# Preparation of out-projection weights tied behind TensorE's products; layer A's weight sums made in place and split a step later

## The chip, the cores and the metric

The kernel runs on one core of a Trainium2 chip. The metric is the device time of one execution in microseconds (us). The engines: PE (TensorE) multiplies, DVE (VectorE) and POOL (GpSimd) do elementwise work, ACT (ScalarE) evaluates functions and copies, SP issues transfers.

## The reference

```python
def recurrent_mixer(h, w_in, conv_w, conv_b, gate_w, gate_b, lam, w_out):   # layer A
    u = jnp.einsum('bsd,dc->bsc', h, w_in)                                  # in-projection
    gate, xb = u[..., :WIDTH], u[..., WIDTH:]
    xb = causal_depthwise_conv(xb, conv_w, conv_b)
    y = rg_lru(xb, gate_w, gate_b, lam)                                     # a scan over the sequence
    return jnp.einsum('bsc,cd->bsd', y * jax.nn.silu(gate), w_out)          # out-projection

def shortconv_mixer(h, w_in, conv_w, w_out):                                # layer B
    u = jnp.einsum('bsd,dc->bsc', h, w_in)                                  # four parts: bg, cg, xv, gate
    y = bg * causal_depthwise_conv(cg * xv, conv_w)
    return jnp.einsum('bsc,cd->bsd', y * jax.nn.silu(gate), w_out)

x = x + recurrent_mixer(rmsnorm(x, g0), ...)
x = x + shortconv_mixer(rmsnorm(x, g1), ...)
return rmsnorm(x, final_g)
```

The model width is 1024, the inner width 1536, the sequence 2048, all in float32.

## The kernel before, in words

**Stages.** Four projections follow one another on PE: A's in-projection (`in_A`), A's out-projection (`outA`), B's in-projection (`in_B`), B's out-projection (`outB`). Each float32 operand is split into two float16 tiles, a high part made by ACT and a remainder made by DVE, and each block product is three matmuls of 128x512 (`mm3`, L497, L500, L501). The sequence is cut into four chunks of 512 columns, called c = 0 to 3.

**Strassen's scheme.** The out-projections, and B's in-projection, use a seven-product scheme (`SEVEN`), which needs sums of weight blocks: S1 = A21 + A22, S2 = S1 - A11, S3 = A11 - A21, S4 = A12 - S2 (`combinations`, L473 and after; the sums themselves run on POOL at L481). The weights of an out-projection are therefore prepared during the in-projection before it and kept in DRAM: `OutSums.weights` loads four raw blocks for each of six k into tiles `wx` (four buffers, L1202), has POOL sum them into `ws` (two buffers, shared with junk of other squares), has `split_w` make the high part `wy` on ACT (L1189) and the remainder on DVE (L1190), and stores it (L1207). Before any of that it must know the scale of the weights: `out_scale` loads the 24 pieces of the whole matrix into `pre` and has ACT square and sum each (L816), then `scale_from` adds up (one small matmul `pt`, then L800 and other small DVE steps).

**How that work is spread.** These preparations are generators in the list `extra`. Each entry is [count, period, generator]; `advance`, called between pieces of the in-projection's products, adds one to the count and runs the generator a step whenever count % period is 0. For A the entry is [-60, 2, ...], for B [-24, 3, ...].

**What sets the order on an engine.** A scheduler orders the instructions of each engine by its own estimate of when each can run, and each engine then executes its list strictly in that order. `after(a, b)` only says that a stands behind b in the scheduler's time; it adds no wait. `pe_last` and `blocks_last` hold the newest product of PE. Many helpers tie their work behind it that way (`z_square`, `inv_between`), `out_scale`, `split_w` and the sums do not.

**in_A.** It goes pair by pair of heads (six pairs). A pair has two units: the first gives the convolution's input (evacuated by ACT L860 and DVE L862 to L871), the second the gate, evacuated by ACT L955 (Tanh) and DVE L956, which also frees the PSUM accumulators `acc` (six buffers, two for each run of 48 matmuls). The scan (`mixer`) runs ACT L908 to L926, POOL L929, DVE L930, and the products `z` go to DRAM through `z_done` (L761) with POOL's differences (L764) in the tiles `u` and `sg`.

**outA and the turn to in_B.** `emitA` takes each finished piece of x, squares it (ACT L226) and adds it to `sa` on POOL (L227). When a chunk c is complete, `endA` defers two steps by 2 and 4 products: the first puts the sum of squares through PE (`ss`, L233), the second broadcasts its inverse root through PE (`pn`, L259; copied to `inv` by ACT L262). `besideA` makes B's operands meanwhile: from product n = 52 it normalizes two of c = 2's eight blocks a step (L302). c = 3 is finished in `second_half`, at the start of in_B: its `ss` and `pn`, then eight L302, then differences and splits by L348, L354, L364, L368 and L310. `unit_scale` for the next unit's weights ends with DVE L394, and the splits L417 (ACT) and L418 (DVE) wait for it.

Of the kernel before, what the change touches and what calls it, by code (L numbers as in the profile page):

```python
# [10 lines left out]
AF = mybir.ActivationFunctionType  # L11
ALU = mybir.AluOpType
# [6 lines left out]
NH = 12  # L19
CH = 512  # L20
HALF = 1024
KB = D // P
# [24 lines left out]
def trunk(ctx, tc, xT, xn, prm, wa, ga, oa, wb, ob, out):  # L47
    nc = tc.nc
    v, s, g, sp = nc.vector, nc.scalar, nc.gpsimd, nc.sync
# [17 lines left out]
    wt = {  # L67
        (l, n, k): dr.tile([P, 2, CH], F16, name=f"w{l}{n}_{k}", tag=f"w{l}{n}_{k}")
        for l, names in (("A", ("S1", "S2", "S3", "S4")), ("B", ("A11", "A12", "A22", "S1", "S2", "S3", "S4")))
        for n in names  # L70
        for k in range(NH // 2)
    }
# [19 lines left out]
    def buf(pool, tag, name, bufs, dt=F32):  # L92
        return pool.tile([P, ROW], dt, tag=tag, name=name, bufs=bufs)[:, 0:CH]

    def pair16(pool, tag, name, bufs):
        t = pool.tile([P, 2, ROW], F16, tag=tag, name=name, bufs=bufs)
        return t[:, :, 0:CH]
# [4 lines left out]
    def two_over(dst, src):  # L102

        v.tensor_scalar(
            out=dst.bitcast(I32), in0=src.bitcast(I32), scalar1=EXP_MASK, scalar2=None,
            op0=ALU.bitwise_xor,
        )
# [4 lines left out]
    def root(dst, src):  # L112

        v.tensor_scalar(out=dst, in0=src, scalar1=TINY, scalar2=None, op0=ALU.max)
        v.tensor_scalar(
            out=dst.bitcast(I32), in0=dst.bitcast(I32), scalar1=1, scalar2=EXP_MASK,
            op0=ALU.logical_shift_right, op1=ALU.bitwise_and,
        )
# [170 lines left out]
    def inv_between(acc, inv, queue=None):  # L289

        ss = ps.tile([P, 4], F32, tag="g", name="ss", bufs=2)[:, 0 : acc.shape[1] // P]
        with tc.high_priority(PR):
            sums_of(acc, ss, pe_last[0])
        if not queue:
            yield
        with tc.high_priority(PR):
            inv_from(ss, inv, queue, s.copy, pe_last[0])
        yield


    def normed(l, x, kk, inv):
        return v.scalar_tensor_tensor(  # L302
            out=x, in0=x, scalar=gs[l][:, kk : kk + 1], in1=inv, op0=ALU.mult, op1=ALU.mult
        )
# [79 lines left out]
    def unit_scale(l, sq, sw, behind=None):  # L384


        pt = ps.tile([P, 4], F32, tag="g", name="pt", bufs=2)
        ins = nc.tensor.matmul(pt, ones, sq, start=True, stop=True)
        if behind is not None:
            after(ins, behind)  # L390
        v.tensor_reduce(out=sw[:, 0:1], in_=pt, axis=AX.X, op=ALU.add)  # L391
        root(sw[:, 1:2], sw[:, 0:1])
        two_over(sw[:, 2:3], sw[:, 1:2])
        v.tensor_scalar(  # L394
            out=sw[:, 2:3], in0=sw[:, 2:3], scalar1=0.5 * W_TOP / ROOT, scalar2=None, op0=ALU.mult
        )
        v.tensor_scalar(
            out=sw[:, 3:4], in0=sw[:, 1:2], scalar1=hs[l], scalar2=ROOT,
            op0=ALU.mult, op1=ALU.mult,
        )  # L400
        return sw
# [74 lines left out]
    def combinations(raw):  # L476


        def wsum(x, y, op):
            t = buf(wp, "ws", "ws", 2)  # L480
            g.tensor_tensor(out=t, in0=x, in1=y, op=op)  # L481
            return t

        a11, a12, a21, a22 = raw
        yield "A11", a11
        s1 = wsum(a21, a22, ALU.add)
        yield "S1", s1
        s2 = wsum(s1, a11, ALU.subtract)
        yield "S2", s2
        yield "A12", a12  # L490
        yield "S4", wsum(a12, s2, ALU.subtract)
        yield "S3", wsum(a11, a21, ALU.subtract)
        yield "A22", a22
# [9 lines left out]
    throttle, pe_last, blocks_last, evac_last = [None, None], [None], [None], [None]  # L503
# [136 lines left out]
    def defer(fn, steps):  # L640
        deferred.append([steps, fn])
# [9 lines left out]
    extra = []  # L651
# [141 lines left out]
    def scale_from(sq, t, behind=None):  # L793


        pt = ps.tile([P, 2 * NH], F32, tag="g", name="pt", bufs=2)[:, 0 : sq.shape[1]]
        ins = nc.tensor.matmul(pt, ones, sq, start=True, stop=True)
        if behind is not None:
            after(ins, behind)
        v.tensor_reduce(out=t[:, 1:2], in_=pt, axis=AX.X, op=ALU.add)  # L800
        root(t[:, 1:2], t[:, 1:2])
        two_over(t[:, 0:1], t[:, 1:2])
        v.tensor_scalar(
            out=t[:, 0:1], in0=t[:, 0:1], scalar1=0.5 * W_TOP / ROOT, scalar2=None, op0=ALU.mult
        )
        v.tensor_scalar(
            out=t[:, 1:2], in0=t[:, 1:2], scalar1=ROOT / W_TOP, scalar2=None, op0=ALU.mult
        )

    def out_scale(wdram, t):  # L810

        sq = wsq
        for i in range(2 * NH):
            b = buf(wp, "ws", "pre", 2)
            sp.dma_start(b, wdram[:, i * CH : (i + 1) * CH])
            s.activation(b, b, AF.Square, accum_out=sq[:, i : i + 1])  # L816
            if i < 2 * NH - 1:
                yield
        scale_from(sq, t)
        yield  # L820

    marks = []
# [256 lines left out]
    def in_order(ins):  # L1079

        if loads:
            after(ins, loads[-1])
        loads.append(ins)

    def after(ins, first):
        tc.add_manual_dep(
            ins.ins, first.ins.name,
            mybir.DependencyInfo(mybir.DependencyClass.NoSync, mybir.DependencyReason.SCHED_ONLY),
            reason="order",
        )  # L1090
# [45 lines left out]
    class OutSums:  # L1136
# [49 lines left out]

        def split_w(self, pool, tag, bufs, a):
            t = pair16(pool, tag, tag, bufs)
            s.activation(t[:, 0, :], a, AF.Copy, scale=self.wsc[:, 0:1])  # L1189
            v.scalar_tensor_tensor(  # L1190
                out=t[:, 1, :], in0=a, scalar=self.wsc[:, 0:1], in1=t[:, 0, :],
                op0=ALU.mult, op1=ALU.subtract,
            )
            return t

        def weights(self, pre):

            yield from pre
            for k in range(KH):
                raw = []  # L1200
                for n in range(4):
                    raw.append(buf(wk, "wx", "wx", 4))  # L1202
                    sp.dma_start(raw[n], self.raw_w(k, n))
                yield
                for name, a in combinations(raw):
                    if (self.l, name, k) in wt:
                        sp.dma_start(wt[self.l, name, k], self.split_w(wk, "wy", 2, a))  # L1207
                        yield
                    if self.l == "A" and name == "S3":
                        break  # L1210

        def load_z(self, half, name, k):
            t = self.raw[half, name, k] = buf(wp, "zr", "zr", 10)
# [166 lines left out]
    for c in range(2):  # L1380
        for i in range(4):
            t = wk.tile([P, D], F32, tag="xn", name="xn", bufs=4)
# [31 lines left out]
    sideA = [second()]  # L1414

    preA, preB = out_scale(oa, wsc[0]), out_scale(ob, wsc[1])

    def follows(l, wdram, t):

        o = OutSums(l, wdram, t)  # L1420

        def start(anchor):
            o.start(anchor)
            extra.append([0, 1, o.ahead()])
        return o, start
# [3 lines left out]
            run(extra.pop(0)[2])  # L1429

    outA, startA = follows("A", oa, wsc[0])
    extra.append([-60, 2, outA.weights(preA)])
    in_A(hA, w0, head, sideA, startA, nothing)
    while sideA:
        advance(sideA)
# [18 lines left out]
    def endA(c, ts):  # L1454
        if c == 3:
            return
        steps = inv_between(sums[c], inv[c // 2][c % 2])
        for n in (2, 4):
            defer(lambda: next(steps, None), n)

    def besideA(n):


        if n in (1, 5):
            raw = []
            u = n // 4
            for q in range(4):
                raw.append(buf(wk, "wx", "wx", 4))
                in_order(sp.dma_start(raw[q], wb[u][:, q * CH : (q + 1) * CH]))
            sws.append(unit_scale(1, *unit_squares(raw), pe_last[0]))  # L1470
        if n >= 32 and n < 36:
            k = n - 32
            for kk, name in ((k, "B11"), (k + 4, "B21")):
                normed(1, xh[0][kk, 0], kk, inv[0][0])
                add(hB[0], name, k, xh[0][kk, 0])
        if n == 35:
            for ks in ((0, 1), (2, 3)):
                early.append(build_h(1, xh[0], inv[0], ks, hB[0], (0,)))
            early.append(unit_weights(1, wb[0], w0, sws[0]))
        if n >= 52:  # L1480
            for kk in range(2 * n - 104, 2 * n - 102):
                normed(1, xh[1][kk, 0], kk, inv[1][0])
        while early and next(early[0], "end") == "end":
            early.pop(0)

    outA.run(emitA, endA, besideA)
    x = xh[1]
    while early:
# [214 lines left out]
```

## Time and profile before

| | |
|---|---|
| median of 3 runs | 1977.35 us (1976.88 to 1980.92) |
| the profiled execution | 1978.52 us, of which span 1976.7 us |
| busy in the span | PE 98%, DVE 65%, ACT 56%, POOL 36% |
| mean granted clock of PE | 0.992 of full speed |
| PE's longest waits | 6.5 us (DVE L956), 5.3 us (at the start), 3.6 us (DVE L871), 3.0 us (POOL L227) |

The table is read from the last row up: PE is busy for nearly the whole span, so what another engine does matters only where PE stands still for it, or runs at a lower clock. The profile has a list of such waits, and a column PEclk in its table by stretches: 1.00 there is 2.4 GHz, 0.50 is 1.2 GHz.

### The profile page before, as it was taken

The numbers are of one execution on the slowest core, as the hardware profiler recorded it, in microseconds if no ns is written. First come the engines' busy times: TensorE is split into PE (matmuls) and PEld (weight loads), VectorE is DVE, ScalarE is ACT, GpSimd is POOL, SyncE is SP. The second block draws the span as 40 slices with busy tenths as digits, with TensorE's granted clock in tenths as the row PEclk, the third lists the DMA queues.
The fourth block names the chain that finished last, engine by engine and source line by source line (L and its number), as shares of the span: only waits on it lengthen the run. The fifth ranks groups of instructions, "written<-read, shape, count | busy, mean of one in ns | idle before, by whom it ended". The sixth has DMA issues, their size and how long they took to land.

```text
span 1976.7 us, 25501 instructions
## 1 busy us (share of the span) xinstructions
PE 1936.4 (98%) x8930; PEld 904.1 (46%) x8930; DVE 1278.6 (65%) x2098; ACT 1099.9 (56%) x1968; POOL 707.6 (36%) x554
## 2 busy tenths in 40 slices
PE   8999989999999999999999999999999999999998
PEld 4444434444444444444444444444444444444446
DVE  7978877866667787979536656647636336544565
ACT  6888768676757563555644454454452443544432
POOL 0023533221212130344553583664553443522221
PEclk9999999999999999999999999999999999999999
DMA  8432442221104985421241241342130030397472
GB/s 300 140 101 86 152 142 88 84 75 48 70 22 175 386 328 181 149 96 59 70 150 37 81 165 43 97 144 72 62 117 28 27 112 27 122 371 247 109 227 86
DMA packets 157713, 250.88 MB, mean 127 GB/s; under 512 B 15248, under 2 KB 58896, under 8 KB 157584
## 3 DMA queue, kind: packets, MB, share of 16 engines
q1 hardware_dynamic: 157360, 248.72, 37.5%
q8 instruction: 70, 1.15, 0.2%
q0 software_dynamic: 224, 0.53, 0.1%
q14 instruction: 59, 0.48, 0.1%
HBM read 171.06 MB, written 78.12 MB: 126 GB/s over the span
## 4 chain that ended last, share of the span: by engine, by line
PE 79%; DVE 3%; DMA 0%; ACT 0%; issue 0%; POOL 0%; SPq 0%; DVEq 0%; ACTq 0%; POOLq 0%
PE acc L497 11%; PE acc L500 11%; PE acc L501 11%; PE p L501 8%; PE p L497 8%; PE p L500 8%; PE r L497 4%; PE r L500 4%; PE r L501 4%; PE pg L904 2%; PE q L500 2%; PE q L501 2%; PE q L497 2%; DVE op L310 1%; PE ss L233 0%; DMA wr<-in_wb 0%
## 5 line engine op out<-in xcount | busy, mean ns | idle before, releaser
L497 PEld LDWEIGHTS <-wc 128*128 128x128 f16 x2096 | 207.8, 99 | 261.4 <-issue 18.3
L500 PEld LDWEIGHTS <-wc 128*128 128x128 f16 x2096 | 205.3, 98 | 265.8 <-issue 32.8
L501 PEld LDWEIGHTS <-wc 128*128 128x128 f16 x2096 | 205.3, 98 | 257.8 <-issue 15.1
L497 PE MATMUL acc<-op,wc 128*128 128x512 f16 x752 | 284.2, 381 | 14.8 <-DVE sg L956 8.7
L497 PE MATMUL p<-op,wc 128*128 128x512 f16 x768 | 290.8, 379 | 1.4 <-ACT wc L417 1.2
L500 PE MATMUL p<-op,wc 128*128 128x512 f16 x768 | 291.1, 379 | 0.0
L501 PE MATMUL p<-op,wc 128*128 128x512 f16 x768 | 290.6, 379 | 0.4 <-DVE wc L418 0.4
L500 PE MATMUL acc<-op,wc 128*128 128x512 f16 x752 | 286.2, 381 | 2.2 <-DVE op L310 2.2
L501 PE MATMUL acc<-op,wc 128*128 128x512 f16 x752 | 286.2, 381 | 0.0
L929 POOL TENSOR_TENSOR u<-fixed,u 128x512 f32<-128x512 f32 x48 | 54.0, 1147 | 347.4 <-ACT fixed L926 347.4
L227 POOL TENSOR_TENSOR sa<-sa,sq 128x512 f32<-128x512 f32 x48 | 71.0, 1480 | 273.1 <-ACT sq L226 225.9
L1294 DVE SCALAR_TENSOR_TENSOR xo<-acc,fixed,xo 128x512 f32<-128x512 f32 (+1 forms) x120 | 85.0, 710 | 113.2 <-PE acc L501 112.3
L418 DVE SCALAR_TENSOR_TENSOR wc<-wr,fixed,wc 128x512 f16<-128x512 f32 x122 | 105.3, 881 | 78.8 <-ACT wc L417 73.5
L418 DVE SCALAR_TENSOR_TENSOR wc<-ws,fixed,wc 128x512 f16<-128x512 f32 x104 | 104.0, 1005 | 80.4 <-ACT wc L417 72.4
L501 PE MATMUL r<-op,wc 128*128 128x512 f16 x384 | 145.5, 379 | 0.0
L500 PE MATMUL r<-op,wc 128*128 128x512 f16 x384 | 145.5, 379 | 0.0
L497 PE MATMUL r<-op,wc 128*128 128x512 f16 x384 | 145.5, 379 | 0.0
L993 POOL TENSOR_TENSOR pb<-pb,cg 128x512 f32<-128x512 f32 x48 | 69.0, 1437 | 188.6 <-DVE fixed L391 101.9
L417 ACT ACTIVATE wc<-wr,fixed 128x512 f16<-128x512 f32 x122 | 83.6, 712 | 82.1 <-DVE fixed L394 79.5
L862 DVE SCALAR_TENSOR_TENSOR u<-acc,fixed,u 128x511 f32<-128x511 f32 (+2 forms) x138 | 100.8, 741 | 43.5 <-ACT u L860 43.5
L379 ACT ACTIVATE junk<-wr 128x512 f32<-128x512 f32 x136 | 84.3, 621 | 31.8 <-DMA wr<-in_wa 16.1
L930 DVE TENSOR_TENSOR_SCAN u<-a,fixed,u 128x512 f32<-128x512 f32 x48 | 78.5, 1638 | 35.4 <-POOL u L929 35.4
(209 smaller groups left out, 3926.9 us busy)
## 6 DMA issues: line engine op xcount, KB each, us to landing
wr<-in_wb SPq DMA_DIRECT2D x104, 256.0 KB, 3.6
zAT<-u SPq DMA_DIRECT2D x48, 256.0 KB, 2.0
zr<-zAT SPq DMA_DIRECT2D x48, 256.0 KB, 5.1
zr<-zBT SPq DMA_DIRECT2D x48, 256.0 KB, 5.1
wr<-in_wa SPq DMA_DIRECT2D x44, 256.0 KB, 4.2
zAB<-sg SPq DMA_DIRECT2D x36, 256.0 KB, 2.0
zr<-zAB SPq DMA_DIRECT2D x36, 256.0 KB, 5.4
zBB<-ed SPq DMA_DIRECT2D x36, 256.0 KB, 2.0
```

The costliest lines, as they stand in the source:

```text
L227: squared[0] = eng.tensor_tensor(out=acc, in0=acc, in1=sq, op=ALU.add)
L379: ins = s.activation(junk, t, AF.Square, accum_out=sq[:, m : m + 1])
L417: last_hi[0] = s.activation(t[:, 0, :], src, AF.Copy, scale=sw[:, 2:3])
L418: v.scalar_tensor_tensor(out=t[:, 1, :], in0=src, scalar=sw[:, 2:3], in1=t[:, 0, :], op0=ALU.mult, op1=ALU.subtract,)
L497: ins = nc.tensor.matmul(acc, wh, xh, start=start, stop=False, **kw)
L500: nc.tensor.matmul(acc, wh, xl, start=False, stop=False, **kw)
L501: return nc.tensor.matmul(acc, wl, xh, start=False, stop=stop, **kw)
L862: v.scalar_tensor_tensor(out=u[:, n:], in0=a[:, 0 : CH - n], scalar=ac(3 - n), in1=u[:, n:], op0=ALU.mult, op1=ALU.add,)
L929: g.tensor_tensor(out=u, in0=w, in1=u, op=ALU.mult)
L930: v.tensor_tensor_scan(out=u, data0=a, data1=u, initial=stA[:, h : h + 1], op0=ALU.mult, op1=ALU.add,)
L993: g.tensor_tensor(out=t, in0=t, in1=cg[m, half, c], op=ALU.mult)
L1294: ins = v.scalar_tensor_tensor(out=x[:, ts], in0=acc[:, ts], scalar=zsc[half][:, 2:3], in1=x[:, ts], op0=ALU.mult, op1=ALU.add,)
```

## The change

Four edits. `now` puts an instruction behind the newest product of PE in the scheduler's time: `out_scale`'s squares, `split_w`'s ACT copy, and A's sums get it, and `scale_from` is given the same and a step of its own. For layer A `sums_only` makes the four sums in place, on POOL, in the tiles of the raw weights (S1 in a22, S3 in a21, S2 in a11, S4 in a12), in two steps of two, and the four splits follow in the next four steps; a k takes seven steps in place of five. `endA` defers 3 and 5 products in place of 2 and 4 for c = 1 and 2. c = 2's blocks are normalized from n = 53, three a step.

```diff
+    def now(ins):
+        last = pe_last[0] or blocks_last[0]
+        if last is not None:
+            after(ins, last)
 ...
-            s.activation(b, b, AF.Square, accum_out=sq[:, i : i + 1])
-            if i < 2 * NH - 1:
-                yield
-        scale_from(sq, t)
+            now(s.activation(b, b, AF.Square, accum_out=sq[:, i : i + 1]))
+            yield
+        scale_from(sq, t, pe_last[0] or blocks_last[0])
         yield
 ...
         def split_w(self, pool, tag, bufs, a):
             t = pair16(pool, tag, tag, bufs)
-            s.activation(t[:, 0, :], a, AF.Copy, scale=self.wsc[:, 0:1])
+            now(s.activation(t[:, 0, :], a, AF.Copy, scale=self.wsc[:, 0:1]))
 ...
                 yield
-                for name, a in combinations(raw):
-                    if (self.l, name, k) in wt:
+                for name, a in self.sums_only(raw) if self.l == "A" else combinations(raw):
+                    if name:
                         sp.dma_start(wt[self.l, name, k], self.split_w(wk, "wy", 2, a))
-                        yield
-                    if self.l == "A" and name == "S3":
-                        break
+                    yield
+
+        def sums_only(self, raw):
+            a11, a12, a21, a22 = raw
+            def to(x, a, b, op):
+                now(g.tensor_tensor(out=x, in0=a, in1=b, op=op))
+            to(a22, a21, a22, ALU.add)
+            to(a21, a11, a21, ALU.subtract)
+            yield None, None
+            to(a11, a22, a11, ALU.subtract)
+            to(a12, a12, a11, ALU.subtract)
+            yield None, None
+            yield from (("S1", a22), ("S3", a21), ("S2", a11), ("S4", a12))
 ...
-    extra.append([-60, 2, outA.weights(preA)])
+    extra.append([-30, 2, outA.weights(preA)])
 ...
-        for n in (2, 4):
+        for n in (3, 5) if c else (2, 4):
 ...
-        if n >= 52:
-            for kk in range(2 * n - 104, 2 * n - 102):
+        if n >= 53:
+            for kk in range(3 * n - 159, min(KB, 3 * n - 156)):
```

Every engine has as many instructions of each kind as before; only their order differs. The start count -30 in place of -60 moves nothing: the period is 2, and count % 2 is 0 for every second step of a negative count too, so in both kernels the generator starts at once.

**ACT, pair hp = 1 of in_A.** Here stand the evacuations L955 of the pair's gate unit, the mixer's L926, and the splits `wy` of the out-projection's weights. Before (L1189 is `split_w`):

```order
L955 ACTIVATE sg<-acc,fixed 128x512
L1189 ACTIVATE wy<-ws,fixed 128x512
L955 ACTIVATE sg<-acc,fixed 128x512
L926 ACT_TABLE_LOAD
L926 ACTIVATE fixed<-fixed 128x1024
L1189 ACTIVATE wy<-ws,fixed 128x512
L786 ACTIVATE fixed<-sg 128x512 x2
L1189 ACTIVATE wy<-ws,fixed 128x512 x2
L379 ACTIVATE junk,fixed<-wr 128x512
L1189 ACTIVATE wy<-ws,fixed 128x512
L955 ACT_TABLE_LOAD
L955 ACTIVATE sg<-acc,fixed 128x512 x2
```

Changed (the changed file has other line numbers: L960 is L955 of before, L931 is L926, L1194 is L1189, L865 is L860):

```order
L931 ACT_TABLE_LOAD
L931 ACTIVATE fixed<-fixed 128x1024
L960 ACT_TABLE_LOAD
L960 ACTIVATE sg<-acc,fixed 128x512 x2
L1194 ACTIVATE wy<-wx,fixed 128x512
L786 ACTIVATE fixed<-sg 128x512 x2
L1194 ACTIVATE wy<-wx,fixed 128x512
L960 ACTIVATE sg<-acc,fixed 128x512 x2
L1194 ACTIVATE wy<-wx,fixed 128x512
L786 ACTIVATE fixed<-sg 128x512 x2
L1194 ACTIVATE wy<-wx,fixed 128x512
L865 ACTIVATE u<-acc,fixed 128x512 x2
```

Of the five splits shown between the first L955 and the last two, two stay ahead of the last two. From the first split of the kernel to that place there were eleven, now there are two; the others come later in in_A, the last in the fifth pair, where before it stood in the fourth.

**POOL, the same place.** L764 are the differences of z, L929 the mixer's products, L481 the sums. Before:

```order
L929 TENSOR_TENSOR u<-fixed,u 128x512 x6
L481 TENSOR_TENSOR ws<-wx 128x512
L764 TENSOR_TENSOR u<-sg 128x512
L481 TENSOR_TENSOR ws<-wx 128x512
L764 TENSOR_TENSOR u<-sg,u 128x512
L764 TENSOR_TENSOR u<-sg 128x512
L481 TENSOR_TENSOR ws<-ws,wx 128x512
L764 TENSOR_TENSOR u<-sg,u 128x512
L481 TENSOR_TENSOR ws<-wx,ws 128x512
L481 TENSOR_TENSOR ws<-wx 128x512
L929 TENSOR_TENSOR u<-fixed,u 128x512 x2
L481 TENSOR_TENSOR ws<-wx 128x512
```

Changed (L934 is L929 of before, L1220 the sums in place):

```order
L934 TENSOR_TENSOR u<-fixed,u 128x512 x6
L1220 TENSOR_TENSOR wx<-wx 128x512 x2
L764 TENSOR_TENSOR u<-sg 128x512 x2
L764 TENSOR_TENSOR u<-sg,u 128x512
L1220 TENSOR_TENSOR wx<-wx 128x512
L764 TENSOR_TENSOR u<-sg,u 128x512
L1220 TENSOR_TENSOR wx<-wx 128x512
L934 TENSOR_TENSOR u<-fixed,u 128x512 x2
L764 TENSOR_TENSOR u<-sg 128x512 x2
L764 TENSOR_TENSOR u<-sg,u 128x512 x2
L1220 TENSOR_TENSOR wx<-wx 128x512 x4
L934 TENSOR_TENSOR u<-fixed,u 128x512 x4
```

In both, the sums share POOL's list with the mixer and the differences. Between the two groups of mixer's products the changed list has four sums, the old one five; the old one has three more at once after the second group, the changed one four, but only behind the four differences.

**PE, the end of outA.** `ss` of c = 2, among the products of S1 (`wv` are its weights; each `acc` takes 18 matmuls). Before:

```order
L497 LDWEIGHTS wv_7112
L497 MATMUL acc_7367<-zs_6872,wv_7112 128x512
L500 LDWEIGHTS wv_7112
L500 MATMUL acc_7367<-zs_6872,wv_7112 128x512
L501 LDWEIGHTS wv_7112
L501 MATMUL acc_7367<-zs_6872,wv_7112 128x512
L233 MATMUL ss_7362<-fixed_310,sa_7071 128x1 x4
```

Changed:

```order
L497 LDWEIGHTS wv_7136
L497 MATMUL acc_7338<-zs_6989,wv_7136 128x512
L500 LDWEIGHTS wv_7136
L500 MATMUL acc_7338<-zs_6989,wv_7136 128x512
L501 LDWEIGHTS wv_7136
L501 MATMUL acc_7338<-zs_6989,wv_7136 128x512
L233 MATMUL ss_7365<-fixed_310,sa_7047 128x1 x4
```

Both pieces stand in the third accumulator of S1: before, `ss` follows its first three matmuls, the 39th of the run; now it follows all 18, the 54th.

## Rows read from the trace of the kernel before

**Rows 1.** The page: busy time, share of the span, instructions.
```profile
PE 1936.4 (98%) x8930; PEld 904.1 (46%) x8930; DVE 1278.6 (65%) x2098; ACT 1099.9 (56%) x1968; POOL 707.6 (36%) x554
```
**Rows 2.** Whom PE waited for: us in total, times, longest us.
```profile
PE acc L497 <- DVE sg L956: 8.7, 2, 6.5
...
PE acc L497 <- DVE u L871: 3.6, 1, 3.6
PE ss L233 <- POOL sa L227: 3.0, 1, 3.0
...
PE pt L388 <- DVE sg L956: 0.9, 1, 0.9
```
**Rows 3.** Stretches: length, busy us (instructions) of PE, PEld, DVE, ACT, POOL; PEclk, DMA, GB/s.
```profile
127.00:129.00 2.00, 0.00 (x0) 0.00 (x0) 2.00 (x5) 0.72 (x2) 1.34 (x2) 1.00 1.04 400
225.00:250.00 25.00, 21.28 (x99) 9.53 (x98) 20.48 (x20) 17.78 (x35) 21.45 (x13) 1.00 0.61 201
250.00:275.00 25.00, 21.87 (x87) 9.29 (x87) 14.98 (x34) 11.96 (x22) 6.70 (x5) 0.86 0.39 131
825.00:850.00 25.00, 22.01 (x95) 10.84 (x94) 20.60 (x25) 12.20 (x22) 15.83 (x11) 0.86 0.34 116
850.00:875.00 25.00, 25.00 (x122) 11.87 (x120) 18.37 (x28) 12.11 (x21) 10.38 (x7) 1.00 0.38 126
875.00:925.00 50.00, 48.34 (x229) 22.15 (x227) 48.95 (x77) 31.00 (x63) 18.71 (x14) 1.00 0.12 37
...
1000.00:1430.00 430.00, 429.81 (x2010) 196.81 (x2009) 251.06 (x346) 204.33 (x396) 235.66 (x187) 1.00 0.29 95
```
**Rows 4.** Timeline of PE after 252: start, us, instruction, [idle before <-releaser].
```profile
252.77 0.59 PE L497 MATMUL acc<-op,wc 128*128 128x512 f16 x1 [6.49 <-DVE sg L956]
...
257.37 0.38 PE L501 MATMUL acc<-op,wc 128*128 128x512 f16 x1
```
**Rows 5.** Timeline of ACT, 245 to 252.
```profile
245.46 0.72 ACT L1189 ACTIVATE wy<-ws,fixed 128x512 f16<-128x512 f32 x1 [3.25 <-POOL ws L481]
247.59 0.72 ACT L1189 ACTIVATE wy<-ws,fixed 128x512 f16<-128x512 f32 x1 [1.41 <-POOL ws L481]
...
251.31 1.27 ACT L955 ACTIVATE sg<-acc,fixed 128x512 f32<-128x512 f32 x2
```
**Rows 6.** Timeline of DVE, 242 to 253.
```profile
242.25 4.25 DVE L930 TENSOR_TENSOR_SCAN u<-a,fixed,u 128x512 f32<-128x512 f32 x2
...
252.03 1.28 DVE L956 SCALAR_TENSOR_TENSOR sg<-sg,acc 128x512 f32<-128x512 f32 x2 [1.25 <-ACT sg L955]
```
**Rows 7.** POOL's instructions by line: names, shapes, count, busy us, mean ns, idle before.
```profile
L227 POOL TENSOR_TENSOR sa<-sa,sq 128x512 f32<-128x512 f32 x48 | 71.0, 1480 | 273.1 <-ACT sq L226 225.9 <-DMA zr<-zAB 44.3 <-DMA xo<-x 2.6
...
L481 POOL TENSOR_TENSOR ws<-wx 128x512 f32<-128x512 f32 x24 | 36.3, 1511 | 36.2 <-ACT junk L379 24.7 <-DMA wx<-in_oa 6.9 <-PE p L501 3.8
```
**Rows 8.** Timeline of PE, 826 to 845, outA's last products.
```profile
826.12 0.38 PE L497 MATMUL acc<-zs,wv 128*128 128x512 f16 x1
...
834.32 0.38 PE L501 MATMUL acc<-zs,wv 128*128 128x512 f16 x1
837.69 1.87 PE L233 MATMUL ss<-fixed,sa 128*128 128x1 f32 x8 [2.99 <-POOL sa L227]
839.42 0.59 PE L497 MATMUL acc<-zs,wv 128*128 128x512 f16 x1
...
844.45 0.38 PE L497 MATMUL acc<-zs,wv 128*128 128x512 f16 x1
```
**Rows 9.** Timeline of POOL, the last addition to c = 2's squares.
```profile
836.00 1.64 POOL L227 TENSOR_TENSOR sa<-sa,sq 128x512 f32<-128x512 f32 x1 [2.02 <-ACT sq L226]
```
**Rows 10.** Timeline of DVE, 879 to 917, start of in_B.
```profile
879.37 5.83 DVE L302 SCALAR_TENSOR_TENSOR xo<-xo,fixed,inv 128x512 f32<-128x512 f32 x8 [0.52 <-ACT inv L262]
...
916.91 0.13 DVE L394 TENSOR_SCALAR fixed<-fixed 128x1 f32<-128x1 f32 x1
```
**Rows 11.** Timeline of PE, 917 to 918.
```profile
917.85 0.39 PE L497 MATMUL p<-op,wc 128*128 128x512 f16 x1 [1.23 <-ACT wc L417]
```

## The prediction

> **What bounds the kernel now.** I read the page's busy times first: PE works for 98% of the span [rows 1], so the change can only win where PE stands still or runs at its lower clock. The list of PE's waits comes next [rows 2]. The reader is to see four of its lines: 8.7 us in two waits for DVE's L956, 3.6 us in one for L871, 3.0 us in one for POOL's L227, and 0.9 us more for L956. Then the table by stretches, for PEclk [rows 3]: 1.00 but for 0.86 in 250 to 275 and in 825 to 850, the stretches behind two of those waits; a stretch at 1.2 GHz follows them. Last come the timelines of the engines named there. Three places matter.
>
> *246 us.* PE stands still for 6.49 us until DVE's L956 frees an accumulator, and then issues 11 matmuls from 252.77 to 257.37, 0.42 us apart [rows 4]. At the full clock 39 matmuls start between 826.12 and 834.32, so one takes 8.20 / 38 = 0.216 us [rows 8]; the 11 lost 4.60 - 11 x 0.216 = 2.2 us. L956 at 252.03 waited for ACT's L955 at 251.31 [rows 5, 6], and L955 stood in ACT's list behind splits L1189, which waited for sums of POOL: 3.25 and 1.41 us at the last of them [rows 5]. So the place costs 6.5 + 2.2 = 8.7 us.
>
> *332 us.* The other wait for L956: 8.7 - 6.5 = 2.2 us [rows 2].
>
> *834 us.* PE reaches c = 2's `ss` after 39 of the S1 products and waits 2.99 us for the last addition to its squares [rows 8, 9]. Afterwards the clock is at the lower level: 12 matmuls from 839.42 to 844.45 cost 5.03 - 12 x 0.216 = 2.4 us too much, and the eight small passes of `ss`, 837.69 to 839.42, half of their 1.73 us, 0.9 [rows 8]. That place costs 3.0 + 3.3 = 6.3 us.
>
> **The change part by part.**
>
> *Layer A's splits and sums.* Nothing is added or removed: 24 sums on POOL, 24 splits on ACT and DVE. The trace has no sum of `wx` in place, but L227 writes over one of its inputs and takes 1480 ns against 1511 for the sums [rows 7], so I take the same duration. What moves is the order. Nine of the eleven splits ahead of the last pair of L955 go: 9 x 0.72 = 6.5 us, and with them the waits of 4.7 us [rows 5]. By that alone L955 would run at 251.3 - 11.2 = 240.1. Two things keep it later: two splits remain ahead of it, and the evacuations before it stand behind the mixer's L926, which has its own chain. I estimate 241 to 243.5. On DVE, L956 follows the two scans (4.25 us together [rows 6]) and two L1190, so it ends at 243 to 246. PE needs the accumulator 6.49 us before 252.77, at 246.28. So the wait goes, and the slow stretch with it; I leave 0.7 us for a remainder: +8.0 us. The ends are +8.7 and, if L956 comes 3 us later than I think and the clock falls again, +3.
>
> *What is late next in A.* The removed splits come back in the third to fifth pair. At 332 us ACT's order up to the awaited L955 is the same as before, its splits ahead are two fewer, and it starts from an earlier end of the second pair: +1.5 of 2.2 us, with ends 2.2 and -2. In the first pair the squares of the raw weights move ahead of an evacuation L860, and both L882 of the pair ahead of an L862, on the chain that ends in the 3.6 us of L871 [rows 2]; each of these costs DVE or ACT 0.6 to 0.7 us. I take -0.8 us, ends +0.5 and -1.7. The splits in the fourth and fifth pair, 13 of them, fall where PE did not wait at all: -0.8 us, ends 0 and -2. Of the 0.9 us that PE waited for L956 at a `pt` [rows 2], in the second pair too, I count +0.6. Layer A together: 8.0 + 1.5 - 0.8 - 0.8 + 0.6 = +8.5 us.
>
> *outA's end.* `ss` of c = 2 now stands after 54 of the S1 products instead of 39. The 15 more take 15 x 0.216 = 3.2 us, from 834.70 (where PE stopped, 837.69 - 2.99) to 837.94; POOL's addition ends at 836.00 + 1.64 = 837.64 [rows 9]. So the wait is covered by 0.3 us, the products themselves being the cover, and in_B would start 6.3 us earlier. If POOL is later by up to 1 us, that much comes back, but a pause so short leaves the clock up, as 2.2 us at 332 did.
>
> *But this gain meets a full DVE.* From 875 to 925 DVE is busy 48.95 of 50 us, against 18.37 of 25 us before it [rows 3]. The stretch runs from the first L302 at 879.37 to L394 at 916.91, 37.5 us [rows 10]; PE stands still for 1.23 us and starts at 917.85, 0.94 us after L394 [rows 11]. L302 waits for `pn` of c = 3. Its place in PE's order is seven matmuls later than before (1.5 us), and PE is 6.3 us earlier, so L302 starts at 879.4 - 6.3 + 1.5 = 874.6. Between L302 and L394 the order has one L540 and one L418 fewer and two L1029 more: as many instructions, 0 to 1.7 us longer, I take 1.0. L394 then comes at 874.6 + 37.5 + 1.0 = 913.1, PE starts at 914.0 and not at 917.85: of 6.3 us 3.8 remain, and PE's wait there grows from 1.2 to about 3.7 us. The ends: 4.8 us if DVE's extra is nothing, and 0 if DVE can't start L302 before 879 because its list before it is as full.
>
> *Does the clock fall after a wait of 3.7 us?* The rows disagree: it fell after 6.49 and after 2.99 us, and stayed at 1.00 in and after the 3.6 us for L871 [rows 2, 3]. I take that it stays, and keep -2.5 us as an end. The Trainium skill (TensorE: Matmul & The Clock Gate, "Why this matters for your kernels") warns against pauses between bursts of matmuls, since TensorE then starts again at the lower clock. By that rule the new wait pays the same price as the old one at 834 us, and the gain at this place shrinks to some 1 us; this case's rows follow the rule at 246 and 834 us and not at the wait for L871.
>
> *The normalizing of c = 2 in threes from n = 53, `ss` of c = 1 18 matmuls later.* PE waited at neither; eight L302 in three steps instead of four are the same work on a DVE that has 6.6 us of idle time in 850 to 875 [rows 3]. I take 0, ends +0.3 and -1.
>
> *B's ties.* The combinations of layer B stay as they are; ACT's squares and splits are ordered a little differently throughout in_B. There PE is busy for 429.81 of 430 us [rows 3], so nothing can be won. I take -0.7 us, ends 0 and -3.
>
> Sum: 8.5 + 3.8 - 0.7 = 11.6 us less than the profiled execution's own 1978.52, 1966.9. That execution was 1.2 us above the median of 1977.35, which gives 1965.7; I forecast 1966.3, between.
>
> **The rivals.**
>
> *The second gain is spent.* DVE can't start L302 earlier, or its 37 us grow, or the clock falls after the longer wait. For it: 48.95 of 50 us busy. Against it: DVE's idle time before 875. The place gives 0 instead of 3.8: 1970.
>
> *The wait at 246 only moves.* The pair's end is freed, but the third pair's L860 then waits for stores of the `u` tiles, which hang on POOL's differences, and these stand beside the same sums. For it: POOL is busy 21.45 of 25 us in 225 to 250 [rows 3]. Against it: the changed order puts the differences ahead of four of the sums. Then A gives 2 to 5 us, not 8.5: 1970 to 1973.
>
> *Slower: POOL's list blocks the mixers.* The sums in place hold the four `wx` buffers until the last split of a k is made, so the next k's raw tiles load later; POOL, strictly in order, then stands at a sum that waits for its load, with the mixer's L929 behind it, and scan, gate, L860 and the accumulators behind that. PE has some 10 us of slack there, as long as a run of 48 matmuls (48 x 0.216). From a delay of 10 us on a k it decides: with 2 to 4 us lost in each of the five later k, and a slow stretch of 2.2 us behind two of them, A loses 8.5 + 14 to 24 us against my sum: 1981 to 1990. Against it: a k has seven steps in place of five, and the sums are tied behind products, so the load has longer.
>
> *It does nothing in A* (the new start count does nothing, and the freed ACT is not what L956 waited for): then only the second place counts, 1974 to 1975. The chain in rows 4 to 6 speaks against it.
>
> **How the numbers follow.** Forecast with both gains, 1961 to 1968.5: 0.50. Second gain spent: 0.17. Wait at 246 moved: 0.13. Nothing in A: 0.08. POOL blocks: 0.12. About 0.2%, 4 us, is what a measurement can tell from no change, so faster ends at 1973.4 and slower begins at 1981.3. Faster: 0.50 + 0.17 + most of 0.13 = 0.77. Same: the rest of that, the case without A and the mild end of POOL: 0.13. Slower: 0.10. The range leaves out a tenth on each side: 1960 to 1977; the forecast's own is 1961 to 1968.5.
>
> **What would show it.** The list of PE's waits after: no 6.5 us for L956, no 3.0 us for L227, a longer wait for the split L417 (or L418) at the start of in_B, 3 to 4 us. PEclk 1.00 from 225 to 275 and in the slice of outA's end. ACT's L955 without waiting splits ahead. I am wrong if a wait for L956 or for L860's chain of over 3 us stands anywhere in the second to fifth pair, if PE waits for `ss` still, or if in_B between 1000 and 1430 has more than 3 us of idle time.

## The result, and the profile after

| | before | changed |
|---|---|---|
| median of 5 runs | 1977.35 us (1975.90 to 1980.92) | 1967.0 us (1965.07 to 1970.29) |
| ratio | | 0.9946, 95% interval 0.9931 to 0.9961 |
| profiled execution | span 1976.7 us, clock 0.992 | span 1963.3 us, clock 0.994 |

The change makes the kernel 10.4 us faster; 1966.3 was forecast. The profiled execution is the fastest of the five, so its span lies 13.4 us under that of before; about 2 us of this lie ahead of 126 us, in the start, which differs from execution to execution of one kernel by as much (the first pair's wait began at 123.5 us here and at 125.4 in another execution of the changed kernel).

PE's longest waits after, the view of [rows 2] (us in total, times, longest; L876 is L871 of before, L961 is L956):

```profile
PE p L497 <- ACT pb L536: 5.1, 1, 5.1
PE acc L497 <- DVE u L876: 4.0, 1, 4.0
...
PE acc L497 <- DVE sg L961: 1.0, 1, 1.0
...
PE ss L233 <- POOL sa L227: 0.3, 1, 0.3
```

Of 8.7 us for L956, 1.0 is left; of 3.0 for `ss`, 0.3. The first line is PE at the start of in_B: 5.1 us where before it waited 1.2, and for another instruction, ACT's L536 in place of the split L417. The stretches, the columns of [rows 3]:

```profile
225.00:250.00 25.00, 25.00 (x119) 11.51 (x118) 16.31 (x20) 15.95 (x27) 17.73 (x14) 1.00 0.57 194
250.00:275.00 25.00, 24.55 (x105) 11.14 (x103) 19.94 (x49) 17.40 (x30) 3.36 (x3) 1.00 0.30 84
825.00:850.00 25.00, 24.72 (x123) 12.15 (x122) 23.47 (x34) 10.05 (x18) 12.52 (x8) 1.00 0.33 114
875.00:925.00 50.00, 44.91 (x204) 20.30 (x203) 44.91 (x69) 27.95 (x55) 19.40 (x18) 0.97 0.18 58
```

PE is busy throughout 225 to 250, and both slow stretches of before (PEclk 0.86) are at 1.00; but 875 to 925, 1.00 before, has 0.97 now.

Timeline of ACT at the place of [rows 5] (L960 is the evacuation L955 of before, L1194 the split L1189):

```profile
231.38 1.28 ACT L960 ACT_TABLE_LOAD   x1
232.67 1.26 ACT L960 ACTIVATE sg<-acc,fixed 128x512 f32<-128x512 f32 x2
233.83 0.72 ACT L1194 ACTIVATE wy<-wx,fixed 128x512 f16<-128x512 f32 x1
235.38 0.63 ACT L786 ACTIVATE fixed<-sg 128x512 f32<-128x512 f32 x1 [0.83 <-DVE sg L887]
...
237.90 0.70 ACT L1194 ACTIVATE wy<-wx,fixed 128x512 f16<-128x512 f32 x1
238.52 1.24 ACT L960 ACTIVATE sg<-acc,fixed 128x512 f32<-128x512 f32 x2
```

The last L955 runs at 238.5 instead of 251.3, and neither split ahead of it waited for a sum. Timeline of PE at outA's end and at the start of in_B, as in [rows 8, 11]:

```profile
825.67 1.05 PE L233 MATMUL ss<-fixed,sa 128*128 128x1 f32 x8 [0.28 <-POOL sa L227]
...
903.21 0.59 PE L497 MATMUL p<-op,wc 128*128 128x512 f16 x1 [5.09 <-ACT pb L536]
903.58 0.63 PE L500 MATMUL p<-op,wc 128*128 128x512 f16 x1
```

and of DVE over the stretch of [rows 10]:

```profile
862.38 6.41 DVE L302 SCALAR_TENSOR_TENSOR xo<-xo,fixed,inv 128x512 f32<-128x512 f32 x8
...
901.33 1.70 DVE L1034 SCALAR_TENSOR_TENSOR cg<-pb,fixed,cg 128x512 f32<-128x512 f32 x2
902.96 0.14 DVE L394 TENSOR_SCALAR fixed<-fixed 128x1 f32<-128x1 f32 x1
```

`ss` takes 1.05 us and not 1.87, so the clock is up there. L302 starts 17.0 us earlier than before, but L394 only 13.9 us: 40.6 us lie between them instead of 37.5. PE restarts 14.6 us earlier, at the lower clock (0.59 and 0.63 us a matmul).

What ends PE's wait is seen in ACT's list, first before, then after:

```profile
917.08 0.72 ACT L417 ACTIVATE wc<-wr,fixed 128x512 f16<-128x512 f32 x1 [7.82 <-DVE fixed L394]
```
```profile
902.47 0.69 ACT L536 ACTIVATE pb<-p,fixed 128x512 f32<-128x512 f32 x1 [3.62 <-DVE cg L1034]
903.13 0.72 ACT L417 ACTIVATE wc<-wr,fixed 128x512 f16<-128x512 f32 x1
```

Before, the split L417 waits for L394, and PE starts at 917.85 behind that split. Now L536, which empties one of PE's accumulators into a tile `pb`, stands ahead of L417, and it waits for DVE's L1034. PE starts at 903.21, when L536 ends; the first L417 has then only begun, so PE did not wait for it.

### The profile page after: what moved, and what is told of

Read it like the earlier page. It is cut to its first block, busy times and chain, and to the rows that moved or that the text cites. A ratio compares the mean times of both kernels' runs of the same rounds, so it can differ in the third digit from the quotient of the medians.

```text
span 1963.3 us, 25473 instructions
## 1 busy us (share of the span) xinstructions
PE 1932.6 (98%) x8930; PEld 903.1 (46%) x8930; DVE 1274.1 (65%) x2098; ACT 1101.7 (56%) x1968; POOL 708.5 (36%) x554
## 3 DMA queue, kind: packets, MB, share of 16 engines
q1 hardware_dynamic: 157360, 248.72, 37.7%
## 4 chain that ended last, share of the span: by engine, by line
PE 77%; issue 11%; DVE 6%; ACT 3%; POOL 2%; DMA 1%; SPq 0%; DVEq 0%; POOLq 0%; ACTq 0%
PE acc L497 11%; PE acc L501 11%; PE acc L500 11%; PE p L497 8%; PE p L500 8%; PE p L501 8%; PE r L497 4%; PE r L501 4%; PE r L500 4%; PE pg L909 2%; PE q L501 2%; PE q L497 2%; PE q L500 2%; DVE op L310 1%; DVE wc L418 1%
## 5 line engine op out<-in xcount | busy, mean ns | idle before, releaser
L934 POOL TENSOR_TENSOR u<-fixed,u 128x512 f32<-128x512 f32 x48 | 51.3, 1090 | 363.3 <-ACT fixed L931 363.3
L418 DVE SCALAR_TENSOR_TENSOR wc<-wr,fixed,wc 128x512 f16<-128x512 f32 x122 | 115.2, 962 | 68.8 <-ACT wc L417 59.7
L418 DVE SCALAR_TENSOR_TENSOR wc<-ws,fixed,wc 128x512 f16<-128x512 f32 x104 | 96.6, 935 | 75.4 <-ACT wc L417 70.7
L998 POOL TENSOR_TENSOR pb<-pb,cg 128x512 f32<-128x512 f32 x48 | 64.3, 1341 | 195.2 <-DVE fixed L391 95.6
L417 ACT ACTIVATE wc<-wr,fixed 128x512 f16<-128x512 f32 x122 | 83.5, 711 | 66.5 <-DVE fixed L394 64.4
L935 DVE TENSOR_TENSOR_SCAN u<-a,fixed,u 128x512 f32<-128x512 f32 x48 | 82.7, 1723 | 37.0 <-POOL u L934 36.9
```

The lines of the kernel that those rows point to most:

```text
L417: last_hi[0] = s.activation(t[:, 0, :], src, AF.Copy, scale=sw[:, 2:3])
L418: v.scalar_tensor_tensor(out=t[:, 1, :], in0=src, scalar=sw[:, 2:3], in1=t[:, 0, :], op0=ALU.mult, op1=ALU.subtract,)
L934: g.tensor_tensor(out=u, in0=w, in1=u, op=ALU.mult)
L935: v.tensor_tensor_scan(out=u, data0=a, data1=u, initial=stA[:, h : h + 1], op0=ALU.mult, op1=ALU.add,)
L998: g.tensor_tensor(out=t, in0=t, in1=cg[m, half, c], op=ALU.mult)
```

## The experiments

All ratios are to the kernel before, run beside each; times are medians.

**1. Layer A's part alone.** The end of outA is put back:

```diff
-        for n in (3, 5) if c else (2, 4):
+        for n in (2, 4):
-        if n >= 53:
-            for kk in range(3 * n - 159, min(KB, 3 * n - 156)):
+        if n >= 52:
+            for kk in range(2 * n - 104, 2 * n - 102):
```

> The changed kernel with the end of A's out-projection as before (steps 2 and 4, normalizing in twos from n = 52); layer A's part of the change kept. Theory (layer A carries nearly all of the gain, the other place gives back what it wins because DVE is full there): the wait for `ss` is back with 3.0 us and a slow stretch behind it, the wait at the start of in_B is back at 1 to 2 us; about 1968 us. Rival (each place gives what the prediction's sum says, 8.5 and 3.8): about 1970.8 us.

1969.58 us, ratio 0.9955 (0.9942 to 0.9967). Waits of PE:

```profile
PE p L497 <- ACT pb L536: 4.2, 1, 4.2
PE acc L497 <- DVE u L876: 4.0, 1, 4.0
PE ss L233 <- POOL sa L227: 3.0, 1, 3.0
```

Layer A's part gives most of the gain; the time lies between the two expectations and rules out neither. But in_B's wait is 4.2 us although the end of outA is as before, where 1 to 2 us were expected. So something else in the change makes that wait longer: the ties of layer B (run 7).

**2. The end of outA alone**, on the kernel before (the diff above the other way round).

> The kernel before with only the end of A's out-projection changed (steps 3 and 5, normalizing in threes from n = 53). Theory: no wait for `ss`, but PE waits 4 to 5.5 us near 912 us at the start of in_B, net gain 0 to 1.5 us: about 1976.3 us, with both waits for L956 as before. Rival (the prediction's 3.8): about 1973.5 us.

1979.74 us, ratio 1.0008 (0.9998 to 1.0017): no gain, where both expectations had one. The waits for L956 are there as before, `ss` still waits (1.87 us, not nothing), and in_B's start has taken the rest:

```profile
PE acc L497 <- DVE sg L956: 8.6, 2, 6.5
...
PE p L497 <- ACT wc L417: 4.0, 1, 4.0
```

The forecast's 3.8 us for this place is refuted for the edit by itself.

**3. The ties, but sums made as before.** `weights` is the old loop over `combinations` again, for both layers; `now` stays on squares and splits.

> The changed kernel with layer A's sums made as before (a new tile each, a split right behind each sum); the ties behind TensorE's products stay. Theory (what counts is how many splits stand in ACT's list ahead of the late L955): four splits stand there instead of eleven, the wait of 6.5 us shrinks to under 1.5 us, about 1968 to 1969 us. Rival (the sums in place and their distance from the splits count, since ACT stood still for POOL's sums): 4 to 6 us of that wait stay, with a slow stretch, 1973 to 1976 us.

1967.68 us, ratio 0.9944 (0.9932 to 0.9956), the whole change's 0.9946 over again. No wait of PE for L956 over 0.4 us is left; the profile's waits are, after those of the start, 5.1 (in_B), 4.0 (first pair) and 1.8 us. Making the sums in place, and a step later, brings nothing that can be measured.

**4. Sums in place, without the ties.** `now` returns at once, `scale_from` gets no anchor.

> The changed kernel without the ties: sums in place and a step later, but the squares, sums and splits not put behind TensorE's products. Theory (the number of splits ahead of L955 counts): the order has eight splits ahead of the late pair of L955, a wait for L956 of 2 to 5 us stays near 246 us, 1971 to 1975 us. Rival (in place is what counts): no such wait, ACT never stands still for a sum, about 1967 to 1968 us.

1996.34 us, ratio 1.0091 (1.0077 to 1.0105): 18 us slower than before, worse than either expectation. PE's waits, then two rows of ACT and two of POOL (L1192 is the split, L1218 the sum in place):

```profile
PE acc L497 <- DVE fixed L869: 16.2, 2, 13.1
```
```profile
249.93 0.72 ACT L1192 ACTIVATE wy<-wx,fixed 128x512 f16<-128x512 f32 x1 [1.27 <-POOL wx L1218]
...
259.90 0.72 ACT L1192 ACTIVATE wy<-wx,fixed 128x512 f16<-128x512 f32 x1 [8.10 <-POOL wx L1218]
```
```profile
258.61 2.62 POOL L1218 TENSOR_TENSOR wx<-wx 128x512 f32<-128x512 f32 x2 [8.71 <-DMA wAS<-wy]
...
288.94 1.27 POOL L1218 TENSOR_TENSOR wx<-wx 128x512 f32<-128x512 f32 x1 [11.89 <-DMA wx<-in_oa]
```

Here is the third rival, alive: the raw tiles are held until their splits are made, POOL stands 8.7 us at a sum whose transfers are late, ACT stands at a split behind POOL with the evacuations L863 behind it, and PE stops for 13.1 us, until 273.9 (POOL's wait of 11.9 us comes after that). The prediction gave it 0.12 and named the tie among what speaks against it; without the ties it happens.

**5. Eight differences at the start of in_B on POOL instead of DVE.**

```diff
-            v.tensor_tensor(out=x[k, 1], in0=x[k + 4, 1], in1=x[k, 1], op=ALU.subtract)
+            eng.tensor_tensor(out=x[k, 1], in0=x[k + 4, 1], in1=x[k, 1], op=ALU.subtract)
-            v.tensor_tensor(out=t2[k], in0=x[k + 4, 0], in1=t2[k], op=ALU.subtract)
+            eng.tensor_tensor(out=t2[k], in0=x[k + 4, 0], in1=t2[k], op=ALU.subtract)
```

> The changed kernel, with eight differences of the last chunks' operands at the start of in_B (L364 and L368) made by POOL instead of DVE. Theory (PE's wait of 5.1 us there is DVE's load between L302 and L394): DVE has 8 x 0.6 = 4.8 us less in that stretch, the wait falls to 0 to 1.5 us and the slow stretch behind it goes, about 1962 to 1963 us. Rival (POOL, at 1.3 to 1.7 us for one, delays the operands or slows DVE beside it by as much as it takes over): 1966 to 1970 us.

1966.12 us, ratio 0.9934 (0.9921 to 0.9946); no clear difference from the change. DVE's instructions from 862 to 903 us, first of the changed kernel, then of this one:

```profile
L310 DVE TENSOR_TENSOR op<-xo,op 128x512 f16<-128x512 f32 x8 | 6.3, 812 | 0.0
```
```profile
L310 DVE TENSOR_TENSOR op<-xo,op 128x512 f16<-128x512 f32 x8 | 11.1, 1433 | 0.0
```
```profile
L368 POOL TENSOR_TENSOR t<-xo,t 128x512 f32<-128x512 f32 x4 | 7.3, 1842 | 4.3 <-DVE op L310 4.3
```

The same eight L310 take 11.1 instead of 6.3 us while POOL works beside them, and L348 and L354 together 8.0 instead of 5.3: of the 6.3 us taken off DVE (L364 and L368 in the changed kernel) at least as much comes back as slower instructions. L394 comes 38.6 us behind L302 instead of 40.6, but PE still waits, some 10 us earlier and for an accumulator that DVE's L540 empties:

```profile
PE q L497 <- DVE pb L540: 4.2, 1, 4.2
```

The rival holds.

**6. A start that acts.** The count of -30 is made to mean something for layer A:

```diff
-            if e[0] % e[1] == 0 and next(e[2], "end") == "end":
+            if (e[0] > 0 or e[1] != 2) and e[0] % e[1] == 0 and next(e[2], "end") == "end":
```

> The changed kernel with a start count that acts: layer A's preparation begins after 30 calls instead of at once. Theory (the squares of the raw weights stand beside the first pair's evacuations): the wait of 4.0 us for L876 in the first pair falls to 2 to 3.6 us; the splits move into later pairs, where the ties keep them behind the evacuations, 0 to 2 us of new waits: 1965.5 to 1967.5 us. Rival (that wait has nothing to do with the squares): 4.0 us stays, 1967 to 1969 us.

1960.02 us, ratio 0.9902 (0.9888 to 0.9915), the fastest of all runs, better than both expectations. Waits:

```profile
PE p L497 <- ACT pb L536: 5.3, 1, 5.3
...
PE acc L497 <- DVE fixed L871: 2.1, 1, 2.1
```

The first squares of the raw weights run at 134.5 us instead of 49.0, so the first pair's wait is 2.1 instead of 4.0 us, and in the second to fifth pair PE waits only once for more than 0.4 us, for 0.7. In_B's wait stays. Counted by PE's products, layer A gives 15.2 us here, 4.9 more than in the changed kernel's profile: 3.4 of them in the first pair, where the clock now stays up too (PEclk 1.00 from 120 to 150 us instead of 0.94), and 1.3 at 332 us, where no wait is left.

**7. Layer B without ties**, layer A's part as in the change, the end of outA as before. `out_scale` and `split_w` call `now` for layer A only.

> Layer A's ties and sums as in the changed kernel; layer B's squares and splits without ties, and the end of A's out-projection as before. Theory (the ties of layer B's squares and splits reorder the start of in_B and made its wait grow from 1.2 to 4.2 us in the run with layer A's part alone): the wait is 1 to 2 us again, 3.0 us for `ss` stays, about 1965 to 1966 us. Rival (in_B's wait grows by itself when PE comes earlier, whatever is tied): 4 us, about 1969 us as in that run.

1966.84 us, ratio 0.9937 (0.9924 to 0.9951). Waits, and the stretch behind `ss`:

```profile
PE ss L233 <- POOL sa L227: 3.0, 1, 3.0
...
PE p L497 <- ACT wc L417: 1.2, 1, 1.2
```
```profile
825.00:850.00 25.00, 24.52 (x119) 11.76 (x120) 22.50 (x33) 10.76 (x19) 12.72 (x8) 1.00 0.28 100
```

and DVE over the stretch of [rows 10]:

```profile
863.49 5.75 DVE L302 SCALAR_TENSOR_TENSOR xo<-xo,fixed,inv 128x512 f32<-128x512 f32 x8 [0.57 <-ACT inv L262]
...
900.93 0.14 DVE L394 TENSOR_SCALAR fixed<-fixed 128x1 f32<-128x1 f32 x1
```

Against run 1 only B's ties are gone, and in_B's wait is 1.2 us again instead of 4.2, for L417 again instead of L536. DVE's stretch is 37.4 us, as before; in run 1 it is 41.2 (867.74 to 908.97). PE's coming earlier in layer A doesn't lengthen the wait. The intervals of the two ratios overlap; that B's ties cost time is shown by the wait, not by the medians.

**8. Layer A's splits tied, nothing else changed.**

```diff
-            s.activation(t[:, 0, :], a, AF.Copy, scale=self.wsc[:, 0:1])
+            ins = s.activation(t[:, 0, :], a, AF.Copy, scale=self.wsc[:, 0:1])
+            if self.l == "A":
+                after(ins, pe_last[0])
```

> The kernel before, with only layer A's splits tied behind TensorE's products (neither squares nor sums nor layer B's). Theory (the splits' tie carries the gain): four splits stand ahead of the late pair of L955 instead of eleven, the wait of 6.5 us falls below 1.5 us, 1967 to 1969 us. Rival (the squares' tie is needed, since it lets the whole preparation begin later): 3 us or more of that wait stay, 1972 to 1976 us.

1965.74 us, ratio 0.9936 (0.9923 to 0.9948). One ordering edge gives the gain of the whole change. PE's waits have no L956 any more; the largest after the start are

```profile
PE acc L497 <- DVE u L871: 3.6, 1, 3.6
PE ss L233 <- POOL sa L227: 3.0, 1, 3.0
...
PE pg L904 <- ACT tg L908: 2.0, 1, 2.0
```

**9 to 12. Combinations, and the change again.** Run 9 is run 7 with run 6's late start, run 10 the same with the changed end of outA, run 11 the kernel before with the late start alone, run 12 the changed kernel unaltered.

> Layer A's ties, sums in place and a start that acts after 30 calls; layer B without ties, the end of A's out-projection as before. Theory (the two gains add: the late start's at the first pair, and the short wait of in_B without B's ties): the wait at the start of in_B is 1.2 us, `ss` waits 3.0 us, the first pair 2.1 us: 1956 to 1960 us. Rival (PE's gain in layer A is given back at in_B, DVE being full there): a wait of 4 to 5 us, 1960 to 1964 us.

> As the run before it in this list, with the end of A's out-projection as in the change. Theory (without B's ties the end's gain is still spent, as in the run with the end alone): no wait for `ss`, 3.5 to 4.5 us at the start of in_B, 1957 to 1961 us, no clear difference from its neighbour. Rival (the prediction's 3.8 us for this place): 1953 to 1956 us.

> The kernel before with one edit: layer A's preparation really begins after 30 calls; no ties, sums as before. Theory (the splits cost only where ACT has no room; later ones fall elsewhere, but still ahead of evacuations): the wait of 6.5 us near 246 us goes, one of 2 to 6 us for L956 comes in the third or fourth pair, 1968 to 1974 us. Rival (the place alone counts, the ties do nothing more): no such wait, 1960 to 1965 us.

> The changed kernel once more, beside the other three: 1965 to 1970 us as measured before. If it lies 5 us or more elsewhere, differences between runs of different calls are not to be trusted to 0.2%.

| run | median us | ratio (95% interval) | in_B's wait | `ss` |
|---|---|---|---|---|
| 9, late, B untied | 1962.55 | 0.9923 (0.9909 to 0.9937) | 1.3 | 3.0 |
| 10, and the end | 1960.20 | 0.9919 (0.9905 to 0.9934) | 4.6 | 1.5 |
| 11, late alone | 1971.76 | 0.9972 (0.9961 to 0.9983) | 1.2 | 3.0 |
| 12, the change | 1965.43 | 0.9942 (0.9928 to 0.9956) | 5.1 | 0.6 |

Run 12 repeats the result. Runs 9 and 10 are alike: what the end of outA saves at `ss`, in_B's start takes back, with B's ties or without. Run 9's waits came as expected, but its median lies 2.5 us above its range; run 10's time came as expected, but `ss` still waits 1.5 us. They are not better than run 6 (the intervals overlap), so the two gains did not add up to anything measurable. Run 11's gain is 5 us of run 6's 19; its wait near 246 us is gone, but others have come, and not where they were expected (the third or fourth pair) but in the second:

```profile
PE pg L904 <- ACT tg L908: 6.5, 2, 4.1
...
PE acc L497 <- DVE fixed L391: 2.1, 1, 2.1
```

The place of the work alone is not enough; with the rest of the change on top it gives the lowest ratio measured, run 6, 0.9902 of before. The splits' tie and the late start with nothing else were not run.

## Why the prediction was right, and where its terms were not

*The wait at 246 us (+8.0 forecast): right, with its mechanism.* Runs 3 and 8 keep the splits' tie and lose the wait, run 4 keeps the sums in place and not the ties, and PE waits for L956 still (4.4 us in two waits) and 13.1 us for L869. L955 came at 238.5, earlier than the 241 to 243.5 estimated (PE was 1.6 us ahead there already); the slow stretch went too. The prediction told the edits of layer A as one and did not say which of them did it: it is the tie of the splits, the smallest. POOL's sums in place took 1637 ns on average, where the 1511 of [rows 7] were assumed; nothing waited for the difference.

*332 us (+1.5 of 2.2): right in size.* 1.0 us is left; in run 12 there are two waits of 2.5 and 0.9 us, so the estimate was optimistic for some executions.

*The first pair (-0.8): the cause right, the size too small.* 3.6 became 4.0 us, and the clock fell behind it, which it had not done before (PEclk 0.94 from 120 to 150 us instead of 1.00: of 30 us 0.12 at half speed, up to 1.8 us). Run 8, with the squares untied, has 3.6 us, run 6, with the squares later, 2.1: the squares' place sets this wait.

*Fourth and fifth pair (-0.8), in_B behind its start (-0.7): too dark.* PE waited in neither; from 1000 to 1430 us it was busy for 429.95 us against 429.81. Layer A gave 10.3 us in the profiled execution (PE was 12.5 us earlier at the 39th S1 product, 834.70 against 825.40 - 3.24 = 822.16, of which 2.2 from before the first pair's wait), and some 8 us in run 12 by the same count of products. The sum had 8.5.

*outA's end (+6.3): right to 0.3 us.* PE waited 0.28 us where 0.3 us were forecast to spare, and the clock stayed up. Taken by its letter, the sign "if PE waits for `ss` still" came true, by this 0.28 us (0.61 in run 12).

*The start of in_B (3.8 of 6.3 to remain): this term failed.* Counted product by product, PE's lead over the kernel before is 12.5 us ahead of outA's end, 18.5 behind it, 14.6 at the wait's end and, behind the slow stretch there, 13.8 (16 products later: 922.10 against 908.34). So of 6.0 us gained 1.2 remain. L302 came where it was forecast (17.0 us earlier: 12.5 + 6.0 - 1.5). What failed is the step from L302 to PE.

First, DVE's stretch to L394 grew by 3.0 us, not 1.0 and not within 0 to 1.7. The ties of layer B do that, which the prediction had booked at -0.7 over all of in_B: the stretch is 40.5 to 41.2 us in the changed kernel and in runs 1, 3, 6 and 12, which have these ties, and 37.4 to 37.7 in the kernel before and in runs 2, 4 and 7 to 11, which don't. The exchange of instructions is not what costs: four L1029 take 4.0 us where two took 2.3, and one L540, one L418 and shorter L1025 give 2.1 back. The lengthening is in instructions that both lists have: twenty L310 take 15.7 us instead of 13.8, four L368 3.6 instead of 2.7, eight L302 6.4 instead of 5.8. POOL has one more product and one more sum in that stretch; that these slow the others, as POOL's work does in run 5, is likely but not shown.

Second, another wait ends last. The prediction followed L394, the split L417 and PE; with B's ties PE waits for L536, and so for DVE's L1034. The forecast sign, a wait of 3 to 4 us for L417 or L418, came as one of 5.1 us for L536. Which of B's ties moves L536 ahead of L417 was not tried.

Third, the clock's fall was kept as an end of the range and not taken: 8 matmuls from 903.21 to 906.57 take 3.36 instead of 8 x 0.216 = 1.73 us.

Without B's ties the term fails too. In run 10 the chain is the forecast one and the stretch 37.7 us, but PE waits 4.6 us for L417: L302 starts 16.1 us earlier than before where PE's lead of 19.6 less 1.5 gives 18.1, because DVE is still at L418 and L540 ahead of it when `inv` is ready. That is close to the case in which the prediction's range for this place ends at 0, and nothing remains: PE's lead is 16.1 us ahead of outA's end and 14.7 behind the wait.

That the total came so close (1966.3 against 1967.0) is partly luck: in the profiled execution layer A gave 1.8 us more than its terms and this place 2.6 us less.

*The rivals.* "The second gain is spent" was the truer account of that place (its 1970 us assumed no more from A). "The wait only moves" and "nothing in A" are refuted by the waits. "POOL blocks the mixers" did not happen in the change and did in run 4. Its sum is wrong in the prediction: 1966.3 + 8.5 + 14 to 24 is 1989 to 1999, not 1981 to 1990; run 4 has 1996.3.

## What to carry to other kernels

Work that is prepared beside a tight pipeline belongs behind the pipeline's own instructions in each engine's list; here one ordering edge on the engine that also frees PE's accumulators was worth the whole change (run 8). When edits come together, look for the one that acts: a start count that does nothing, sums in place that are harmful by themselves, and a gain at one place that the next full engine takes back all looked like parts of one success. And a wait saved ahead of a stretch in which another engine is full is not saved time until that engine gets less to do; and moving work from it to an engine that slows it, as in run 5, doesn't give it less.

## What the runs showed of the hardware

The same wait did not always have the same price. `ss` waited 2.98 us in run 1 and in run 7; first run 1's row, then run 7's:

```profile
826.12 1.87 PE L233 MATMUL ss<-fixed,sa 128*128 128x1 f32 x8 [2.98 <-POOL sa L227]
```
```profile
824.26 1.05 PE L233 MATMUL ss<-fixed,sa 128*128 128x1 f32 x8 [2.98 <-POOL sa L227]
```

In run 1 the matmuls came back at the lower clock, in run 7 at the full one. The first pair's wait of 3.6 us did so too; the stretch around it in run 2, then in run 8:

```profile
120.00:150.00 30.00, 26.43 (x108) 11.45 (x107) 22.23 (x47) 22.40 (x46) 5.43 (x4) 0.94 0.45 140
```
```profile
120.00:150.00 30.00, 26.43 (x114) 11.91 (x113) 21.21 (x44) 21.27 (x45) 5.44 (x4) 1.00 0.46 140
```

At 4.0 us PEclk was under 1.00 there in all six profiles that have that wait, at 2.1 us and less in none of the four. But elsewhere 2.03 us were enough: in run 8 PE waits so long for L908, and the matmuls come back at 0.63 us, from 181.92 us on:

```profile
180.00:185.00 5.00, 4.05 (x10) 1.55 (x11) 5.00 (x11) 4.80 (x8) 3.71 (x3) 0.69 0.58 218
```

So the prediction's "a pause so short leaves the clock up" does not hold in general. The falls worked out in this document cost 1.6 to 3.3 us, which is of the size of the scatter between executions of one kernel (the changed kernel's ranged from 1965.07 us at a mean clock of 0.994 to 1970.29 at 0.991). The Trainium skill (TensorE: Matmul & The Clock Gate, "Why this matters for your kernels") warns of such pauses between matmuls. From the first pair on, the waits of 4.0 us and more agree with it; those of 3.6 and 2.98 us do in some profiles and not in others.

DVE's eight L310 took 1433 instead of 812 ns on average beside POOL's differences (run 5). The prediction had counted instructions of the stretch at one duration, whoever works beside them.
